# Inverse roots of the norms element by element on every partition, instead of column sums, a Newton chain on eight columns and a diagonal

## The chip, the cores and the metric

The kernel runs on one core of a Trainium2 chip. The metric is the device time of one execution in microseconds; the median of three runs of the kernel before is 2151.62 us (2151.5 to 2153.11). TensorE (PE) multiplies matrices and writes its results to PSUM banks of 128 partitions by 512 float32; PEld is its weight load, which overlaps the matmuls. VectorE (DVE) and ScalarE (ACT) read those banks and do everything element by element. GpSimd (POOL) makes a few masks at the start. SyncE's queue (SP) issues nearly all transfers, some come from ACT's queue. Each engine runs its own instructions in order and waits on semaphores for the others. Products are made in float32r with operands split into a high and a low part (three matmuls for one product); a few matmuls are float32, which the trace records as two passes.

## The reference

One decoder layer on x of 2048 rows by 1024 columns, then a final norm. Every norm has the form of `rmsnorm`:

```
def rmsnorm(x, w, eps=EPS):
    inv = lax.rsqrt(jnp.mean(x * x, axis=-1, keepdims=True) + eps)
    return x * inv * w

u    = rmsnorm(x, norm_mix_w);  proj = u @ w_in          # hq, hf, hi, hg, attention q k v
mix  = [hgrn2 heads (4), sliding-window attention heads (8)]
h    = x + mix @ w_out
v    = rmsnorm(h, norm_ffn_w)
h    = h + (silu(conv(v @ w_gate)) * (v @ w_up)) @ w_down
out  = rmsnorm(h, final_norm_w)
```

The number `inv` belongs to a row of x (a token). The kernel holds x transposed, features on partitions and tokens on the free axis, so a norm needs a sum over partitions, and its result is wanted in two forms: spread over all partitions along the token axis (`invb`, to multiply a transposed product), and as a column with tokens on partitions (`rs`, to scale the product v, which comes out with tokens on partitions).

## The kernel before, in words

The 2048 tokens are done in two halves of 1024. Each half goes through: the products k and v of attention (`kv`, two `unit`s of 48 matmuls), an interleaved stretch of HGRN2 heads and attention heads (`hgrn`, `attend`, `project_v`, in the order of the list `ORDER`), the output projection (`out_proj`, tiles `pop`), the gated MLP (`gate_up`, pairs of units by a Strassen-Winograd scheme in `pair_unit`, tiles X, Y, Z), and the down projection (`down`, tiles `pdx`, `pdy`), at whose end the next half's x is loaded (`load`) and its `kv` units begin. Around all of it a planner with a cost model of each instruction sorts the program into one order per engine; code that is written in one place can stand elsewhere in the order, and `tc.issue_after` pins some of it.

`Stats` holds the norms. Its accumulator `acc` (tiles `invb` or `sums`, 128 partitions by 1024 or 512 tokens) takes the squares of the features: ACT squares, DVE adds (line 251). Then, in before:

- `inverse` (from line 262): for each block of 128 tokens a float32 matmul with the accumulator's block as weights and one column of ones as the moving side gives 128 sums in one column of a bank `pst` (line 271); `rsqrt` (lines 169 to 181) makes the inverse root of those 8 (or 4) columns by a bit trick and three Newton steps, 11 small DVE instructions; line 279 multiplies the identity matrix by the columns, which puts 128x128 diagonals into the accumulator.
- `spread` (line 289): a float32 matmul of a matrix of ones with those diagonals puts each inverse root on all partitions (bank `pinv`), and ACT copies it to SBUF (line 292).

This happens nine times for whole, half or quarter accumulators: x of the first half (in `head`), h of each half (in `gate_up`, at products S4 and A22 of the first pair), the final norm of the first half's two column halves (`o2` while the down projection's last product P4 runs, `o` in the next half's `kv` units), x of the second half (`xs`, in the same units), and the second half's final norm at the very end (`o2`, `o`, `o`). ACT's functions live in tables, and a change to another table is an instruction of its own (`ACT_TABLE_LOAD`); Identity, Copy and Square run under any.

PSUM is handed out from three groups: `mm` (4 banks), `hg` (2) and `at` (2). Line 196 makes the low part `wlo` of a weight tile, which the third of each three matmuls of a `unit` needs. Line 1201 scales the finished output tiles h before line 1202 writes them out. Line 716 scales the product v by `rs`.

Of the kernel before, what the change touches and what calls it, by code (L numbers as in the profile page):

```python
# [8 lines left out]
F32 = mybir.dt.float32  # L9
# [31 lines left out]
UT = 7  # L41
# [12 lines left out]
def hymba_layer(ctx: ExitStack, tc: tile.TileContext, a: dict, out: bass.AP):  # L54
# [18 lines left out]
    def ps(kind, name):  # L73
        return spaces[kind].tile([P, 512], F32, tag=kind, name=name)
# [160 lines left out]
    class Stats:  # L235
# [26 lines left out]
        def inverse(self, keep, last=None):  # L262
# [12 lines left out]
            if last is not None:  # L275
# [4 lines left out]
                                    ident.unsqueeze(1).to_broadcast([P, nt, P]),  # L280
                                    rs.unsqueeze(2).to_broadcast([P, nt, P]), op=ALU.mult)

        def spread(self, bank=None):

            n = self.acc.shape[-1]
            w = min(n, 512)
            for b in range(n // w):
                pb = ps(aux[b % 2 if bank is None else bank], "pinv")[:, 0:w]
                marks["pinv"] = nc.tensor.matmul(pb, ones, self.acc[:, b * w:(b + 1) * w], start=True, stop=True)
                if bank is not None:  # L290
                    return pb
                nc.scalar.copy(self.acc[:, b * w:(b + 1) * w], pb)
# [25 lines left out]
    def head(X):  # L318


        st = Stats(inv_tile())
        raw = [raw4(None) for _ in range(3)]
        W = [tuple(wp.tile([P, D], F32R, tag=t, name=f"w{t}", bufs=2) for t in ("hi", "lo")) for _ in range(2)]
        xt = [slot("x") for _ in range(KT)]
        k0, k1, k2 = slice(0, P), slice(P, 4 * P), slice(4 * P, D)
        v0, v1 = slice(0, 2 * P), slice(2 * P, D)
        nc.sync.dma_start(raw[0][:, k0], a["w_att"][ATT_J][:, k0])
        for c in (k1, k2):
            fetched = nc.scalar.dma_start(raw[0][:, c], a["w_att"][ATT_J][:, c])
        with tc.issue_after(fetched.ins):  # L330
            nc.scalar.activation(warm, ones[:, 0:1], AF.Sigmoid)
        for kt in range(KT):
            for c in [h for _, h in halves()] if kt == 0 else [slice(0, HALF)]:
                nc.sync.dma_start(xt[kt][:, c], a["xT"][kt, :, c])
            if kt == 1:
                nc.sync.dma_start(raw[1], a["w_att"][ATT_J + 1])
        nc.sync.dma_start(raw[2], a["w_f"][0])
        o = [[ps("mm", f"kv{b}") for b in range(NB)] for _ in range(2)]
        on_act, on_pe = [], []

        def turn(f, *args):

            with tc.issue_after(on_act[-1].ins) if on_act else ExitStack():
                on_act.append(f(*args))

        def tile_of_x(kt):
            X.append(new_x())
            for c in [h for _, h in halves()] if kt == 0 else [slice(0, HALF)]:
                turn(split_w, xt[kt][:, c], nmw[:, kt:kt + 1], [t[:, c] for t in X[kt]])

        def split_w(src, w, dst):
            h, l = dst
            r = nc.scalar.activation(h, src, AF.Identity, scale=w)
            nc.vector.scalar_tensor_tensor(l, src, w, h.bitcast(F32), op0=ALU.mult, op1=ALU.subtract)
            return r

        def step(u, kt):

            hi, lo = [t[:, kt * P:(kt + 1) * P] for t in W[u]]
            xh, xl = X[kt]  # L360
            with tc.issue_after(on_pe[-1].ins) if on_pe else ExitStack():
                for w, x, f, l in ((hi, xh, kt == 0, False), (hi, xl, False, False), (lo, xh, False, kt == KT - 1)):
                    for b, bs in halves():
                        r = nc.tensor.matmul(o[u][b], w, x[:, bs], start=f, stop=l)
                on_pe.append(r)

        turn(cut, *W[0], raw[0], k0)
        tile_of_x(0)
        step(0, 0)
        turn(cut, *W[0], raw[0], k1)  # L370
        tile_of_x(1)
        step(0, 1)
        turn(cut, *W[0], raw[0], k2)
        turn(cut, *W[1], raw[1], v0)
        for kt in range(2):
            step(1, kt)
        for kt in range(2, KT):
            tile_of_x(kt)
            if kt == 2:
                turn(cut, *W[1], raw[1], v1)  # L380
            else:
                turn(st.square, xt[kt - 3])
            for u in range(2):
                step(u, kt)
        F = tuple(hp.tile([P, D], F32R, tag="m", name=f"w{t}", bufs=KT) for t in ("hi", "lo"))
        turn(cut, *F, raw[2], slice(0, D))
        for kt in range(KT - 3, KT):
            turn(st.square, xt[kt])
        summed = st.last
        with tc.issue_after(on_act[-1].ins), tc.issue_after(summed.ins):  # L390
            constants()
        with tc.issue_after(on_pe[-1].ins):
            st.inverse("x")
        with tc.issue_after(marks["pst"].ins):
            f0 = unit(F, X, "f", kind="aux", then={4: st.spread}, behind={4: "pinv"})
        return o, st.acc, st.rs, f0, summed

    def first_unit(X, i, then={}, kind="mm"):
        return unit(a["w_att"][ATT_J + i], X, "kv", kind=kind, then=then)
# [544 lines left out]
    def gate_up(hf, ops, hs, nxt, last, p):  # L944

        acts = {op: [dp.tile([P, n, 512], F32, name=f"act{hf}{op}{i}") for i, n in enumerate(PIECES)] for op in OPS}
        lo, hi = slice(0, 512), slice(512, HALF)
        invb = hs.acc
        srcs = [w[2 * pr:2 * pr + 2] for pr in range(FT // 2) for w in (a["w_gate"], a["w_up"])]
        for pr in range(FT // 2):  # L950
            f0 = 2 * pr
# [14 lines left out]
            def flush():  # L966
                while later:
                    later.pop(0)()

            later = []  # L970
            then = {"S4": lambda: hs.inverse("h"), "A22": lambda: (hs.spread(), flush())} if pr == 0 else {}
            if pr == 0:
                def behind_first(copied):
                    nonlocal nxt
# [50 lines left out]
    def down(hf, kept, acts, p):  # L1025
# [4 lines left out]
        lo, hi = slice(0, 512), slice(512, HALF)  # L1030
        final = hf + 1 == NH
        NP = len(PIECES)
        todo = [(name, w, t, j) for name, w, t in PRODUCTS for j in range(NP)]
        S = {}

# [79 lines left out]
        for k, (name, _, _, j) in enumerate(todo):  # L1115
            if k + 2 < len(todo):
                ready[k + 2] = prep_piece(k + 2)
            if j == 0:
                if name == "P1":
                    bx = o = [ps("mm", "pdx") for _ in range(4)]  # L1120
                elif name in ("P5", "P2"):
                    by = o = [ps(aux[d % 2], "pdy") for d in range(4)]
                else:
                    o = by if name == "P3" else bx
                if name == "P3":
                    acc = inv_tile() if final else wp.tile([P, HALF], F32, tag="raw", name="sums", bufs=RAW)
                    s1, s2 = [Stats(acc[:, bs], lambda: p.tile([P, 512], F32, tag="ut", name="fsq", bufs=UT))
                              for bs in (lo, hi)]
                if name == "P2" and not final:
                    stage = iter(("xh2", "xl2") * (KT // 2))  # L1130
                    loading = load(hf + 1, X, lambda: p.tile([P, HALF], F32, tag=next(stage), name="x", bufs=6))
            if not final and k >= end - 3:
                xs = next(loading, xs)
            if final and k == end:
                break
            if k == end + 1:
                s2.inverse("o2")
            elif k == end + 3:
                s2.spread()
                finish(hf, hh, s2, hi, [nc.sync])  # L1140
            for d in range(4):
                product(k, o[d], d)
            if j + 1 < NP:
                continue
            for d in range(4):
                h1, h2 = hh[d], hh[d + 4]
                if name in ("P1", "P2"):
                    add(h1[:, lo], o[d])
                elif name in ("P6", "P3"):
                    add(h1[:, hi], o[d])  # L1150
# [12 lines left out]
        if final:  # L1163
# [26 lines left out]
            steps[1][0].inverse("o", last)  # L1190
            finish(hf, hh, steps[1][0], steps[1][1], [nc.scalar, nc.sync], steps[1][0].spread(1))
            return None
        kv = [first_unit(X, 0, {3: lambda: s1.inverse("o"), 7: lambda: xs.inverse("x")}, "aux")]
        kv.append(first_unit(X, 1, {2: lambda: (s1.spread(), finish(hf, hh, s1, lo, [nc.sync])), 4: xs.spread}))
        f0 = unit(a["w_f"][0], X, "f")
        return X, kv, xs.acc, xs.rs, f0

# [103 lines left out]
```

## Time and profile before

| | |
|---|---|
| median of 3 runs | 2151.62 us (2151.5 to 2153.11) |
| the profiled execution's own time | 2152.56 us |
| its span (first to last instruction) | 2150.8 us |
| PE busy | 2136.1 us, 99% of the span |
| DVE busy | 1662.3 us, 77% |
| ACT busy | 1091.3 us, 51% |
| granted TensorE clock, mean | 0.999 |
| DMA, mean busy share of 16 engines | 34.5% on SP's queue, 0.8% on ACT's |

In rows of a timeline the columns are the start in us, the length in us (of all instructions merged into the row), engine, line, operation, output<-inputs, the shape of the array, of the moving side and type, and how many were merged; in brackets stands the idle time of the engine before it and what ended it. Matmuls overlap: a row's length is longer than the distance to the next row's start, and it is the distance that counts. The rows that carry the argument stand in the prediction.

### The profile page before, as it was taken

The numbers are of one execution on the slowest core, as the hardware profiler recorded it, in microseconds if no ns is written. First come the engines' busy times: TensorE is split into PE (matmuls) and PEld (weight loads), VectorE is DVE, ScalarE is ACT, GpSimd is POOL, SyncE is SP. The second block draws the span as 40 slices with busy tenths as digits, with TensorE's granted clock in tenths as the row PEclk, the third lists the DMA queues.
The fourth block names the chain that finished last, engine by engine and source line by source line (L and its number), as shares of the span: only waits on it lengthen the run. The fifth ranks groups of instructions, "written<-read, shape, count | busy, mean of one in ns | idle before, by whom it ended". The sixth has DMA issues, their size and how long they took to land.

```text
span 2150.8 us, 28224 instructions
## 1 busy us (share of the span) xinstructions
PE 2136.1 (99%) x10752; PEld 1786.6 (83%) x10752; DVE 1662.3 (77%) x2450; ACT 1091.3 (51%) x1858; POOL 6.0 (0%) x28
## 2 busy tenths in 40 slices
PE   9999999999999999999999999999999999999998
PEld 7888888888888888888888888888888888888888
DVE  6557888798887878785864688878978788887766
ACT  6456566564444445335734576646544444443353
POOL 1000000000000000000000000000000000000000
PEclk9999999999999999999999999999999999999999
DMA  4111112513232235964631111215223323269643
GB/s 158 49 40 40 42 37 69 164 48 132 86 126 93 97 114 171 380 222 157 214 129 41 46 42 40 64 38 174 84 93 101 110 91 122 92 205 398 224 137 133
DMA packets 94383, 258.04 MB, mean 120 GB/s; under 512 B 11416, under 2 KB 17576, under 8 KB 94248
## 3 DMA queue, kind: packets, MB, share of 16 engines
q1 hardware_dynamic: 88992, 251.30, 34.5%
q10 hardware_dynamic: 5256, 4.94, 0.8%
q8 instruction: 84, 1.38, 0.3%
q14 instruction: 51, 0.42, 0.1%
HBM read 195.10 MB, written 57.15 MB: 117 GB/s over the span
## 4 chain that ended last, share of the span: by engine, by line
PE 79%; ACT 2%; DVE 2%; issue 1%; DMA 0%; ACTq 0%; DVEq 0%
PE X L896 7%; PE X L898 7%; PE X L897 7%; PE pop L217 6%; PE pdx L1109 4%; PE pdx L1107 4%; PE Y L898 4%; PE Y L897 4%; PE Y L896 4%; PE pdx L1108 4%; PE pdy L1109 3%; PE pdy L1108 3%; PE pdy L1107 3%; PE f L217 2%; PE hq L217 2%; PE q L217 2%
## 5 line engine op out<-in xcount | busy, mean ns | idle before, releaser
L721 ACT CAST whi<-raw 128x1024 fp32r<-128x1024 f32 x88 | 92.6, 1053 | 110.3 <-PE X L897 67.6
L897 PE MATMUL X<-T,whi 128*128 128x512 f32 x352 | 137.0, 389 | 0.0
L896 PE MATMUL X<-T,whi 128*128 128x512 f32 x352 | 137.0, 389 | 0.0
L898 PE MATMUL X<-T,wlo 128*128 128x512 f32 x352 | 136.9, 389 | 0.0
L991 DVE SCALAR_TENSOR_TENSOR y<-ga,cw,y 128x1024 f32<-128x1024 f32 x88 | 112.3, 1277 | 26.0 <-ACT y L989 25.9
L903 ACT COPY u<-X 128x512 f32<-128x512 f32 x88 | 51.4, 584 | 133.0 <-PE X L898 132.6
L722 DVE TENSOR_TENSOR wlo<-raw,whi 128x1024 fp32r<-128x1024 f32 x88 | 107.0, 1215 | 0.0
L195 ACT CAST whi<-raw 128x1024 fp32r<-128x1024 f32 x57 | 59.7, 1051 | 87.1 <-PE hq L217 37.1
L196 DVE TENSOR_TENSOR wlo<-raw,whi 128x1024 fp32r<-128x1024 f32 x57 | 69.4, 1217 | 43.3 <-ACT whi L195 42.8
L722 DVE TENSOR_TENSOR xld<-raw,xhd 128x1024 fp32r<-128x1024 f32 x72 | 80.5, 1129 | 19.8 <-ACT xhd L721 19.4
L721 ACT CAST xhd<-raw 128x1024 fp32r<-128x1024 f32 x72 | 69.6, 977 | 43.5 <-DMA raw<-act0T 13.9
L217 PE MATMUL pop<-XL,whi 128*128 128x512 f32 x256 | 88.6, 392 | 0.0
L217 PE MATMUL pop<-XH,wlo 128*128 128x512 f32 x256 | 87.7, 391 | 0.0
L217 PE MATMUL pop<-XH,whi 128*128 128x512 f32 x256 | 86.4, 393 | 0.0
L897 PEld LDWEIGHTS X<-T,whi 128*128 128x128 f32 x352 | 66.1, 188 | 13.7
L898 PEld LDWEIGHTS X<-T,wlo 128*128 128x128 f32 x352 | 66.1, 188 | 13.7
L896 PEld LDWEIGHTS X<-T,whi 128*128 128x128 f32 x352 | 66.0, 188 | 13.7
L1107 PE MATMUL pdx<-xhd,hid 128*128 128x512 f32 x192 | 74.5, 392 | 1.6 <-ACT hid L721 1.0
L619 DVE TENSOR_TENSOR QK<-QK,f 128x1024 f32<-128x1024 f32 x56 | 68.5, 1224 | 8.1 <-ACT G L605 7.7
L1108 PE MATMUL pdx<-xld,hid 128*128 128x512 f32 x192 | 74.7, 389 | 0.0
L1109 PE MATMUL pdx<-xhd,lod 128*128 128x512 f32 x192 | 73.8, 389 | 0.0
L896 PE MATMUL X<-T,Sh 128*128 128x512 f32 x176 | 68.7, 391 | 1.5 <-ACT s L903 1.5
(385 smaller groups left out, 6413.1 us busy)
## 6 DMA issues: line engine op xcount, KB each, us to landing
wr<-in_w_down SPq DMA_DIRECT2D x90, 512.0 KB, 5.4
raw<-in_w_gate SPq DMA_DIRECT2D x44, 512.0 KB, 3.7
raw<-in_w_up SPq DMA_DIRECT2D x44, 512.0 KB, 3.6
raw<-act0T SPq DMA_DIRECT2D x20, 512.0 KB, 8.2
raw<-act1T SPq DMA_DIRECT2D x20, 512.0 KB, 8.3
act0B<-y SPq DMA_DIRECT2D x33, 256.0 KB, 3.2
act1B<-y SPq DMA_DIRECT2D x33, 256.0 KB, 2.3
raw<-in_w_out SPq DMA_DIRECT2D x16, 512.0 KB, 5.1
```

Of the source, the lines that this page charges most:

```text
L196: nc.vector.tensor_tensor(lo, raw, hi.bitcast(F32), op=ALU.subtract)
L217: marks["unit"] = nc.tensor.matmul(o[b], w, x[:, bs], start=f, stop=l)
L619: done = nc.vector.tensor_tensor(own, own, Fv.rearrange("p b w -> p w b").unsqueeze(3).to_broadcast([P, 2, nb, m]), op=ALU.mult)
L721: return (nc.scalar.copy(h, src), (eng or nc.vector).tensor_tensor(l, src, h.bitcast(F32), op=ALU.subtract))
L722: (eng or nc.vector).tensor_tensor(l, src, h.bitcast(F32), op=ALU.subtract))
L896: nc.tensor.matmul(o, wh[:, ws], xh, start=i == 0 and not more, stop=False, skip_group_check=more)
L897: nc.tensor.matmul(o, wh[:, ws], xl, start=False, stop=False, skip_group_check=more)
L898: r = nc.tensor.matmul(o, wl[:, ws], xh, start=False, stop=i == 3, skip_group_check=more)
L991: nc.vector.scalar_tensor_tensor(y, g[:, w:w + HALF], C.cw[:, ft, w:w + 1], y, op0=ALU.mult, op1=ALU.add)
L1107: nc.tensor.matmul(o, wh[:, i, c], ah[:, i, cols], start=f, stop=False, skip_group_check=more)
L1108: nc.tensor.matmul(o, wh[:, i, c], al[:, i, cols], start=False, stop=False, skip_group_check=more)
L1109: nc.tensor.matmul(o, wl[:, i, c], ah[:, i, cols], start=False, stop=l, skip_group_check=more)
```

## The change

Two new functions of `Stats`. `everywhere` replaces `inverse` and `spread` in six of the nine places (x, h of both halves, and `o2`, `o` and `xs` between the halves; the last three at the program's end stay as they were). For each block of 512 tokens: one float32 matmul of ones with the accumulator itself gives the sums on all partitions (bank `psum`), ACT reads the bank and makes the inverse root of every element by a table function (`Abs_reciprocal_sqrt`), DVE reads the bank for the scaled sum, ACT squares the root, and two DVE instructions do one Newton step and leave the result in the accumulator. The planner makes DVE's read of the bank (line 300) wait for ACT's (line 299). `column` makes the column form `rs` for v: it writes partition 0 of the result to DRAM (4 KB) and reads it back with tokens on partitions, 128 partitions by 8 numbers of 4 bytes each. Line numbers in after are 22 to 30 higher from there on.

```diff
+        def column(self):
+            n = self.acc.shape[-1]
+            rs = self.rs = sp.tile([P, n // P], F32, tag="rs", name="rs")
+            row = dp.tile([1, n], F32, name="row")
+            nc.sync.dma_start(row, self.acc[0:1])
+            nc.sync.dma_start(rs, row.rearrange("o (c t) -> (o t) c", t=P))
+
+        def everywhere(self, part, kinds):
+            n = self.acc.shape[-1]
+            for b in range(n // 512):
+                a = self.acc[:, b * 512:(b + 1) * 512]
+                s = ps(kinds[b % 2], "psum")
+                marks["psum"] = nc.tensor.matmul(s, ones, a, start=True, stop=True)
+                y, t = part("y"), part("t")
+                nc.scalar.activation(y, s, AF.Abs_reciprocal_sqrt, scale=1.0 / D, bias=eps)
+                nc.vector.tensor_scalar(a, s, -0.5 / D, -0.5 * EPS, op0=ALU.mult, op1=ALU.add)
+                nc.scalar.activation(t, y, AF.Square)
+                nc.vector.tensor_tensor(t, t, a, op=ALU.mult)
+                nc.vector.scalar_tensor_tensor(a, t, 1.5, y, op0=ALU.add, op1=ALU.mult)
...
         with tc.issue_after(on_pe[-1].ins):
-            st.inverse("x")
-        with tc.issue_after(marks["pst"].ins):
-            f0 = unit(F, X, "f", kind="aux", then={4: st.spread}, behind={4: "pinv"})
+            st.everywhere(lambda name: slot(name)[:, 0:512], aux)
+            st.column()
+        with tc.issue_after(marks["psum"].ins):
+            f0 = unit(F, X, "f", kind="aux")
...
-            then = {"S4": lambda: hs.inverse("h"), "A22": lambda: (hs.spread(), flush())} if pr == 0 else {}
+            then = {"S4": lambda: hs.everywhere(ring, ("mm", "mm")), "A22": flush} if pr == 0 else {}
...
             if k == end + 1:
-                s2.inverse("o2")
+                s2.everywhere(ring, aux)
             elif k == end + 3:
-                s2.spread()
                 finish(hf, hh, s2, hi, [nc.sync])
...
-        kv = [first_unit(X, 0, {3: lambda: s1.inverse("o"), 7: lambda: xs.inverse("x")}, "aux")]
-        kv.append(first_unit(X, 1, {2: lambda: (s1.spread(), finish(hf, hh, s1, lo, [nc.sync])), 4: xs.spread}))
+        kv = [first_unit(X, 0, {3: lambda: s1.everywhere(ring, aux), 7: lambda: (xs.everywhere(ring, aux), xs.column())}, "aux")]
+        kv.append(first_unit(X, 1, {2: lambda: (finish(hf, hh, s1, lo, [nc.sync]))}))
```

Counted over the program, PE loses 40 of its 50 `pst` matmuls on columns of ones and turns 10 `pinv` matmuls into 10 `psum` matmuls of the same shape; ACT loses 10 copies of 128x512 and gains 10 inverse roots, 10 squares and 5 table loads (38 instead of 33); DVE loses 66 small instructions and the diagonals (line 279, four of 128x1024 and two of 128x512) and gains 30 of 128x512; SP gains 4 transfers.

The order moves in three places that the prediction speaks of. First PE in the head, behind the last `kv` matmul (tile `f` is the first HGRN2 unit); before:

```order
L364 MATMUL kv_144<-XH,wlo 128x512
L364 MATMUL kv_145<-XH,wlo 128x512
L271 MATMUL pst<-ones,invb 128x1 x8
L217 MATMUL f_385<-XH,whi 128x512
L217 MATMUL f_386<-XH,whi 128x512
```

and now:

```order
L386 MATMUL kv_144<-XH,wlo 128x512
L386 MATMUL kv_145<-XH,wlo 128x512
L297 MATMUL psum<-invb,ones 128x512 x2
L217 MATMUL f_383<-XH,whi 128x512
L217 MATMUL f_384<-XH,whi 128x512
```

The two sums over all partitions stand where the eight columns stood, and the two `pinv` matmuls that stood after 24 of the 48 `f` matmuls are gone. ACT at the same place (`lbe` is a small softmax for the forget gates, `kT` and `vT` get their bias after DVE has scaled them); before:

```order
L195 CAST whi<-raw 128x1024 x2
L156 ACT_TABLE_LOAD
L156 ACTIVATE lbe<-lbe 128x8
L292 COPY invb<-pinv 128x512 x2
L419 ACTIVATE kT<-kT,battn 128x512
L419 ACTIVATE vT<-vT,battn 128x512
```

and now:

```order
L195 CAST whi<-raw 128x1024 x2
L299 ACT_TABLE_LOAD
L299 ACTIVATE y<-psum,warm 128x512
L156 ACT_TABLE_LOAD
L156 ACTIVATE lbe<-lbe 128x8
L301 ACTIVATE t<-y 128x512
L299 ACT_TABLE_LOAD
L299 ACTIVATE y<-psum,warm 128x512
L301 ACTIVATE t<-y 128x512
L442 ACTIVATE kT<-kT,battn 128x512
L442 ACTIVATE vT<-vT,battn 128x512
```

The exponential for `lbe` stands between the two roots, so there are three table loads where there was one. Then DVE shortly before the second half's `kv` units (`gad` is the last weight piece of the down projection, `h ... sums` the scaling of finished output, `XL` a low part of x, `wlo` the low part of the first `kv` unit's weights); before:

```order
L722 TENSOR_TENSOR gad<-wr,gad 128x512
L232 SCALAR_TENSOR_TENSOR XL<-x,nmw,XH 128x1024
L179 TENSOR_TENSOR t<-y 128x4
L251 TENSOR_TENSOR invb<-invb,x 128x1024
L180 TENSOR_TENSOR t<-t,ms 128x4
L196 TENSOR_TENSOR wlo<-raw,whi 128x1024
```

and now:

```order
L745 TENSOR_TENSOR gad<-wr,gad 128x512
L1230 TENSOR_TENSOR h_7160<-h_7160,sums 128x512
L1230 TENSOR_TENSOR h_7162<-h_7162,sums 128x512
L1230 TENSOR_TENSOR h_7164<-h_7164,sums 128x512
L1230 TENSOR_TENSOR h_7166<-h_7166,sums 128x512
L1230 TENSOR_TENSOR h_7168<-h_7168,sums 128x512
L1230 TENSOR_TENSOR h_7170<-h_7170,sums 128x512
L1230 TENSOR_TENSOR h_7172<-h_7172,sums 128x512
L1230 TENSOR_TENSOR h_7174<-h_7174,sums 128x512
L232 SCALAR_TENSOR_TENSOR XL<-x,nmw,XH 128x1024
L251 TENSOR_TENSOR invb<-invb,x 128x1024
L196 TENSOR_TENSOR wlo<-raw,whi 128x1024
```

The eight scalings of `o2`, which followed the `kv` unit's start before, now stand ahead of that unit's `wlo`. On SP the two transfers of `column` stand behind the third of four loads of `w_v` in the head and behind the second in the second half; and the eight output writes of `o2` now stand ahead of the second half's loads of `w_f` and `w_q`. In the MLP and the down projection's beginning the planner sorts many rows anew (which of two ready products PE takes first), with the same instructions.

More of the change, by code (lines that the diff above doesn't have):

```diff
@@ L948, in gate_up, with ring @@
         invb = hs.acc
+        def ring(name):
+            return p.tile([P, 512], F32, tag="ut", name=name, bufs=UT)
         srcs = [w[2 * pr:2 * pr + 2] for pr in range(FT // 2) for w in (a["w_gate"], a["w_up"])]
@@ L1032, in down, with ring @@
         NP = len(PIECES)
+        def ring(name):
+            return p.tile([P, 512], F32, tag="ut", name=name, bufs=UT)
         todo = [(name, w, t, j) for name, w, t in PRODUCTS for j in range(NP)]
```

## The prediction

> **What bounds the kernel now.** First the page, then the busy times by stretch, then the rows around each norm. Page, parts 1 and 2:
>
> ```profile
> span 2150.8 us, 28224 instructions
> PE 2136.1 (99%) x10752; PEld 1786.6 (83%) x10752; DVE 1662.3 (77%) x2450; ACT 1091.3 (51%) x1858; POOL 6.0 (0%) x28
> PEclk9999999999999999999999999999999999999999
> ```
>
> PE works 2136.1 of 2150.8 us at an unthrottled clock. Only time on PE counts: what an edit takes out of PE's order is gained, what makes PE wait is lost. Busy times by stretch (its length, then each engine's time and instructions) for the first MLP and the `kv` units between the halves:
>
> ```profile
> 445.00:860.00 415.00, 414.27 (x1832) 342.27 (x1831) 347.93 (x451) 186.96 (x269) 0.00 (x0) 1.00 0.34 110
> 1070.00:1100.00 30.00, 30.00 (x140) 24.20 (x139) 22.86 (x55) 8.50 (x12) 0.00 (x0) 1.00 0.40 141
> ```
>
> PE idles 0.73 of 415 us in the MLP and none of 30 where the next half begins. The sums by columns therefore lie on the path, with nothing that hides them. The head's PE rows, none with an idle time in brackets:
>
> ```profile
> 30.91 1.84 PE L271 MATMUL pst<-ones,invb 128*128 128x1 f32 x16
> 32.61 0.72 PE L217 MATMUL f<-XH,whi 128*128 128x512 f32 x2
> 33.17 0.63 PE L217 MATMUL f<-XL,whi 128*128 128x512 f32 x2
> 33.64 0.62 PE L217 MATMUL f<-XH,wlo 128*128 128x512 f32 x2
> 34.09 0.62 PE L217 MATMUL f<-XH,whi 128*128 128x512 f32 x2
> ...
> 38.20 1.88 PE L289 MATMUL pinv<-invb,ones 128*128 128x512 f32 x4
> 39.51 1.03 PE L217 MATMUL f<-XH,whi 128*128 128x512 f32 x2
> 40.38 0.62 PE L217 MATMUL f<-XL,whi 128*128 128x512 f32 x2
> ```
>
> Two `f` matmuls take 0.455 (33.64 to 34.09), one 0.227. From 30.91 to 33.17 lie eight `pst` matmuls (16 records) and two `f`: the eight cost 2.26 - 0.455 = **1.80**. From 38.20 to 40.38 two `pinv` and two `f`: 2.18 - 0.455 = 1.73 for a pair. Half an accumulator, at the second half's start:
>
> ```profile
> 1077.03 1.02 PE L289 MATMUL pinv<-sums,ones 128*128 128x512 f32 x2
> 1077.48 0.79 PE L217 MATMUL kv<-XH,whi 128*128 128x512 f32 x1
> 1078.11 0.40 PE L217 MATMUL kv<-XL,whi 128*128 128x512 f32 x1
> ...
> 1082.88 0.95 PE L271 MATMUL pst<-ones,sums 128*128 128x1 f32 x8
> 1083.69 0.49 PE L217 MATMUL kv<-XL,whi 128*128 128x512 f32 x1
> 1084.02 0.40 PE L217 MATMUL kv<-XH,wlo 128*128 128x512 f32 x1
> ```
>
> Four `pst` cost 1.14 - 0.23 = **0.91**, a single `pinv` 1.08 - 0.23 = 0.85.
>
> **The change, part by part.** *PE.* Removed are 40 `pst` matmuls: eight each for x, h, h and xs, four each for `o2` and `o`: 4 x 1.80 + 2 x 0.91 = **9.0 us**, at places without a PE wait. The ten `psum` have the shape of the ten `pinv` and the same grouping (pairs for x and h, singles for `o2`, `o`, xs): 0.
>
> *The MLP's wait.* PE stands still once per half in the first MLP pair:
>
> ```profile
> 459.55 0.39 PE L898 MATMUL X<-B,wlo 128*128 128x512 f32 x1
> 460.67 0.50 PE L896 MATMUL X<-T,Sh 128*128 128x512 f32 x1 [0.73 <-ACT s L903]
> PE X L896 <- ACT s L903: 1.5, 2, 0.7
> ```
>
> The product S2T2 goes on in bank X, which ACT must copy first, and nothing stands between. In the new order ten Z and two Y matmuls stand there, 12 x 0.227 = 2.7 us, more than the copy needs: **-1.5** in all. Bounds: 0 if another wait takes its place, -1.5.
>
> *Head, ACT and DVE.* The roots are made later than PE's `f` begins, so the question is whether `vT` and the `kv` banks are ready when `f` ends.
>
> ```profile
> 30.65 1.05 ACT L195 CAST whi<-raw 128x1024 fp32r<-128x1024 f32 x1 [0.30 <-PE kv L364]
> 31.72 1.28 ACT L156 ACT_TABLE_LOAD   x1
> 33.01 0.21 ACT L156 ACTIVATE lbe<-lbe 128x8 f32<-128x8 f32 x1
> 39.25 0.58 ACT L292 COPY invb<-pinv 128x512 f32<-128x512 f32 x1 [6.03 <-PE pinv L289]
> 41.23 0.71 ACT L419 ACTIVATE vT<-vT,battn 128x512 f32<-128x512 f32 x1
> 39.87 0.69 DVE L418 TENSOR_TENSOR kT<-kv,invb 128x512 f32<-128x512 f32 x1 [3.02 <-ACT invb L292]
> ```
>
> ACT read a `pinv` bank 1.05 after its matmul began (39.25 - 38.20), so the first `psum` is there at 31.96. A pass of 512 columns costs ACT 0.58 to 0.71; the new root has no row, I take 0.65 and 0.6 for the square. Then: load to 33.24, root 33.9, load 35.2, `lbe` 35.4, square 36.0, load 37.3, root 37.95, square 38.55. DVE, at 0.65 an instruction, waits for ACT at each step and reaches the first `kT` at 40.1, beside 39.87 before; the first `vT` has its bias at 42.1. PE, with the pair done at 30.91 + 1.73, ends `f` at 32.64 + 48 x 0.227 = 43.5 and takes `vT` then: 1.4 us to spare, so **0**. If the root costs twice the row, the slack is still not used up.
>
> *h.* Per half ACT works 1.28 + 2 x 1.25 - 2 x 0.58 = 2.6 us more, DVE makes six passes of 512 in place of eleven small instructions and the diagonal. The same stretch shows what hides it:
>
> ```profile
> 454.59 0.59 ACT L903 COPY u<-X 128x512 f32<-128x512 f32 x1 [4.99 <-PE X L898]
> 465.22 2.50 DVE L962 TENSOR_TENSOR ga<-ga,invb 128x512 f32<-128x512 f32 x4 [2.75 <-ACT invb L292]
> ```
>
> ACT had 4.99 us idle there and DVE stood 2.75 us waiting for the spread root, which now comes without a second trip over PE: **0**. Line 300, which waits for ACT's load and root, holds up on DVE the low parts of the last T4 operand and of the next unit's weights; in the new order both are due some 5 us later on PE. Were the cover gone, the `Sl` of the second unit would be late next, whose turn on PE I put 2.8 us after it is ready.
>
> *Between the halves.* Here the cover is thin. DVE scales `o2`'s eight output tiles ahead of the weights of the first `kv` unit:
>
> ```profile
> 1059.13 2.19 ACT L231 ACTIVATE XH<-x,nmw 128x1024 fp32r<-128x1024 f32 x2 [3.26 <-DMA x<-in_xT]
> 1062.79 0.68 DVE L722 TENSOR_TENSOR gad<-wr,gad 128x512 fp32r<-128x512 f32 x1
> 1066.65 1.23 DVE L196 TENSOR_TENSOR wlo<-raw,whi 128x1024 fp32r<-128x1024 f32 x1 [0.26 <-ACT whi L195]
> 1071.36 0.39 PE L217 MATMUL kv<-XH,whi 128*128 128x512 f32 x1
> 1078.70 4.90 DVE L1201 TENSOR_TENSOR h<-h,sums 128x512 f32<-128x512 f32 x8 [0.76 <-ACT sums L292]
> ```
>
> The table load and root put ACT's casts 1.9 us back; its 3.26 us of waiting for x swallow that, and I put `gad`'s end at 64.3 (63.5 before). Then 4.9 for `h` and three passes of 128x1024 (`XL`, `invb`, `wlo`) at 1.2, as long as the `wlo` row: `wlo` is ready at 1072.8. PE starts `kv` at 1071.3 and needs it at the fifth matmul, 1072.2. A wait of about **+0.5**; bounds 0 (casts not pushed back) and 2 (the whole push of 1.9 arrives). Behind it the chain is shorter than before: two trips over PE are one, so `kv`'s banks come free before `hq` asks for them, and `w_f` and `w_q` wait about 2 us behind eight writes but are cast 12 us later: 0.
>
> *Column form.* SP stands still until the root is made, writes, waits for the landing, and reads; behind it wait the loads of the last `w_v` pieces and of `w_g`. In the head that is from about 42 to 46, in the second half from about 1101.
>
> ```profile
> L716 ACT ACTIVATE v<-pvv,y x16: 677/687/702, 80.7 to 1183.5; 128x512 f32<-128x512 f32 x16
> 26.36 34.27 SPq L187 DMA_DIRECT2D raw<-in_w_v  x4
> 1145.48 0.69 ACT L716 ACTIVATE v<-pvv,y 128x512 f32<-128x512 f32 x1 [0.43 <-PE pvv L715]
> q10 hardware_dynamic: 5256, 4.94, 0.8%
> odd<-moved ACTq DMA_DIRECT2D x8, 112.0 KB, 2.3
> ```
>
> First use is at 80.7 and 1145.5; the fourth `w_v` load goes out only at 60.6 anyway. ACT's queue moved 5256 packets in 0.8% of 16 x 2150.8 us, 52 ns each; 1024 pieces of 4 bytes at that price take 3.3 us over 16 engines: **0**.
>
> *Sum.* -9.0 - 1.5 + 0.5, and +0.6 for a wait like the MLP's that the new order may bring elsewhere (estimate: one of 0.73): **-9.4**. The profiled execution took 2152.56, so 2143.2; it stood 0.94 above the median, so **2142.2** against 2151.62. With its bounds: -11 (MLP's wait gone, no new one) to -7 (2 at `kv`, 2 elsewhere): 2140.6 to 2144.6.
>
> **Rivals.** *Late chains* (ACT and DVE late at the head and at `kv`): the covers are 1.4 us in the head and none at `kv`. If the root takes ACT as long as a load (1.28) and each hand-over costs 0.3, two roots and six hand-overs make 1.3 + 1.8 = 3.1 late, 1.7 waited in the head, and 2 more at `kv`: 2142.2 + 3.7 = **2146**. For it: strict order on DVE, where line 300 waits for ACT. Against: the copy that ends at 39.83 releases `kT` at 39.87, a hand-over of 0.04.
>
> [...]
>
> *The planner's new order eats the gain.* It was sorted for other durations; in the first MLP PE idles 0.73 us of 415, so the old order left nothing. If the reordered third of each MLP (four pairs and the change to the down projection) brought a 0.73 wait in six places per half, 8.8 us go: **2151**. Against: the order before, by the same planner, had one.
>
> *Slower: the 4-byte read stands in a line.* If its 1024 pieces run on one engine instead of 16, 52 ns x 1024 = 53 us, the column lands at about 98 and 1156 instead of before 80.7 and 1145.5; ACT, in order, stands still at line 716 some 17 and 15 us, PE soon after behind full banks. At 15 each: 2142.2 + 30 = **2172**. It decides from some 35 us of landing on. Against: 112 rows of 1 KB landed in 2.3 us, so a transfer with partitions outermost does spread. [...]
>
> **How the numbers follow.** Forecast 0.72, late chains 0.13, drain 0.03, eaten gain 0.07, slow read 0.05. 0.2% (4.3 us, about what this measurement tells from no change) is passed below 2147.3. Faster: 0.70 of the forecast, 0.11 of the late chains, 0.03 of the drain, 0.84; same: 0.02, 0.02 and 0.06 of the eaten gain, 0.10; slower: its last 0.01 and the slow read's 0.05. The range, 2139.5 to 2147.5, takes in the forecast's bounds and the late chains.
>
> **What would show it.** Right: PE busy about 2127, no `pst` before the tail, 38 table loads, the wait on `s` gone in the first pair of both MLPs, a short PE wait for `wlo` at `kv`. Wrong: PE waits in the head for `vT` or a `kv` bank (late chains; ACT gaps after the loads: the drain), waits scattered over the MLP, or ACT idle before the scaling of v for want of `rs` (slow read).

## The result: 0.24% slower, with the time lost in the pace of matmuls that the change does not touch

The changed kernel takes 2157.57 us in the median of 11 runs (2156.53 to 2158.7); the kernel before, run beside it, 2152.59 us (11 runs, 2151.5 to 2153.73). The ratio is 1.0024, 95% interval 1.0015 to 1.0033. Forecast were 2142.2 us, a gain of 9.4; the range ended at 2147.5. It came out 5 us slower instead, some 15 us beside the forecast.

The page of the changed kernel, parts 1 and 2, and the first stretch that the prediction showed of before (length, then busy time and instructions of PE, PEld, DVE, ACT, POOL, granted clock, DMA share, GB/s):

```profile
span 2156.6 us, 28063 instructions
PE 2143.6 (99%) x10672; PEld 1778.8 (82%) x10672; DVE 1666.3 (77%) x2408; ACT 1104.2 (51%) x1873; POOL 6.4 (0%) x28
PEclk9999999999999999999999999999999999999999
...
445.00:860.00 415.00, 414.24 (x1799) 337.25 (x1798) 346.68 (x442) 188.25 (x270) 0.00 (x0) 1.00 0.33 110
```

PE has 80 records fewer (40 float32 matmuls of two passes each), as the change says, and yet 7.5 us more busy time. In the MLP it is as busy as before, 414.24 of 415 us at clock 1.00, and gets through 1799 matmuls where it got through 1832. (Eight of the 33 fewer come with the change of instructions and of their places in the order: the same instructions at the old addresses, below, have 1824. The other 25 are lost pace.) So no wait took the gain; the matmuls themselves follow each other more slowly. PE's waits of the changed kernel (line waited for: us in total, times, longest) agree:

```profile
PE pdx L1137 <- ACT xhd L744: 1.3, 2, 0.8
...
PE kv L217 <- DVE wlo L196: 0.3, 1, 0.3
```

The two waits of 0.73 for `s` are gone, the short one for `wlo` has come (0.3 where 0.5 was forecast), and nothing on the list is near 15 us.

Where the pace is lost shows when groups of one operation are laid side by side (busy us, mean ns of one). First before, then the changed kernel:

```profile
L896 PE MATMUL X<-B,whi 128*128 128x512 f32 x176 | 68.5, 389 | 0.0
L896 PE MATMUL Y<-T,Sh 128*128 128x512 f32 x176 | 68.5, 389 | 0.0
L897 PE MATMUL X<-T,Sh 128*128 128x512 f32 x176 | 68.5, 389 | 0.0
```

```profile
L919 PE MATMUL X<-B,whi 128*128 128x512 f32 x176 | 69.3, 394 | 0.0
L919 PE MATMUL Y<-T,Sh 128*128 128x512 f32 x176 | 69.3, 394 | 0.0
L920 PE MATMUL X<-T,Sh 128*128 128x512 f32 x176 | 68.7, 391 | 0.0
```

The same three products, the same shape and count: two take 394 ns instead of 389, the third 391. A matmul has two operands, its weights and its moving operand; here the moving operand is a block of the MLP's input (B) or a sum of blocks (T), of which the rows give the letter alone. The slow ones are those whose moving operand (B11, T1, B21) lies in the pool that is opened for the MLP, its "second homes"; the operands T2, T3, T4 and B22 lie in the first homes, the pool of x. The sum needs the distance between starts rather than the length. A stretch of product Y (start us, length us) in the changed kernel:

```profile
599.66 0.39 PE L919 MATMUL Y<-T,Sh 128*128 128x512 f32 x1
599.89 0.40 PE L920 MATMUL Y<-T,Sh 128*128 128x512 f32 x1
600.13 0.39 PE L921 MATMUL Y<-T,Sl 128*128 128x512 f32 x1
600.36 0.40 PE L919 MATMUL Y<-T,Sh 128*128 128x512 f32 x1
600.60 0.39 PE L920 MATMUL Y<-T,Sh 128*128 128x512 f32 x1
600.83 0.40 PE L921 MATMUL Y<-T,Sl 128*128 128x512 f32 x1
601.06 0.39 PE L919 MATMUL Y<-T,Sh 128*128 128x512 f32 x1
601.29 0.40 PE L920 MATMUL Y<-T,Sh 128*128 128x512 f32 x1
```

Seven distances make 1.63 us, 233 ns each, where the prediction reckoned with 227.

What differs is an address, that is, the byte at which a tile starts in each partition of SBUF, the memory in which the kernel's tiles lie. The new code needs fewer small tiles (the column roots of x, h and the final norm go, the column form `rs` comes), so the pool `small` shrinks from 768 to 640 bytes a partition, and each pool opened after it starts 128 bytes earlier. In the built programs the second homes start at byte 141120 before (64 modulo 256) and at 140992 in the changed kernel (192 modulo 256); first homes and weights stay at 64 modulo 256 in both (weights that lie in a second home move with it). Of the 8340 float32r matmuls of 512 columns, 48 have a moving operand and weights that are not a multiple of 256 bytes apart before the change, and 2172 after it.

### The profile page after: what moved, and what is told of

It reads as the page before. It is cut to its first block, busy times and chain, and to the rows that moved or that the text cites. A ratio compares the mean times of both kernels' runs of the same rounds, so it can differ in the third digit from the quotient of the medians.

```text
span 2156.6 us, 28063 instructions
## 1 busy us (share of the span) xinstructions
PE 2143.6 (99%) x10672; PEld 1778.8 (82%) x10672; DVE 1666.3 (77%) x2408; ACT 1104.2 (51%) x1873; POOL 6.4 (0%) x28
## 2 busy tenths in 40 slices
DMA packets 96466, 258.04 MB, mean 120 GB/s; under 512 B 13498, under 2 KB 19658, under 8 KB 96332
## 4 chain that ended last, share of the span: by engine, by line
PE 80%; ACT 1%; DVE 1%; DMA 1%; issue 0%; ACTq 0%; DVEq 0%
PE X L920 7%; PE X L919 7%; PE X L921 7%; PE pop L217 6%; PE Y L920 4%; PE Y L919 4%; PE Y L921 4%; PE pdx L1137 3%; PE pdx L1139 3%; PE pdx L1138 3%; PE pdy L1137 3%; PE pdy L1138 3%; PE pdy L1139 3%; PE q L217 2%; PE f L217 2%; PE g L217 2%
## 5 line engine op out<-in xcount | busy, mean ns | idle before, releaser
L920 PE MATMUL Z<-B,whi 128*128 128x512 f32 x176 | 69.5, 395 | 0.0
```

The source lines that it names most:

```text
L920: nc.tensor.matmul(o, wh[:, ws], xl, start=False, stop=False, skip_group_check=more)
```

## The experiments

Three theories were open. **Placement:** a 512-column matmul is slower when its moving operand and its weights are not a multiple of 256 bytes apart. **Order:** the planner's new order of the matmuls costs PE its pace. **Contention:** the added ACT work and table loads do. In each kernel with a widened tile every engine's instructions stand in the same order as in the kernel that it was made from, and nothing is computed differently.

### The changed kernel, put back on its old addresses

```diff
-        ms = sp.tile([P, n], F32, tag=f"ms{n}", name="ms")
+        ms = sp.tile([P, n + 16 * (n == 8)], F32, tag=f"ms{n}", name="ms")[:, 0:n]
```

> The changed kernel with one tile of the small pool widened by 64 bytes a buffer (two buffers), so that the pools opened after it, the second-home operands of the MLP among them, start 128 bytes later: at the address that they had before the change. Every engine's instructions stand in the same order as in the changed kernel. Placement theory (a 512-column matmul is slower when its moving operand and its weights stand 128 bytes apart modulo 256; 2172 such matmuls in the changed kernel, 48 before): each goes back from about 233 to 226.7 ns from start to start, 2172 x 6.5 ns = 14.1 us less, 2157.6 - 14.1 = 2143.5 us, which is also the forecast of the prediction (2142.2) within 1.5 us; the MLP products of the page fall from 390 to 389 ns a matmul. Rival, order theory (the planner's new order of the matmuls is what costs PE its pace): the order is the same, so the time stays 2157.6 us. Rival, contention theory (the added ACT work and table loads take the pace from PE): 2157.6 us too.

Measured: 2142.01 us (5 runs, 2141.48 to 2142.64) beside 2152.05 of before (20 runs); ratio 0.9953, interval 0.9939 to 0.9966. Its page, its MLP stretch, the groups of above, and the same stretch of product Y:

```profile
span 2140.1 us, 28063 instructions
PE 2127.5 (99%) x10672; PEld 1778.2 (83%) x10672; DVE 1666.2 (78%) x2408; ACT 1105.6 (52%) x1873; POOL 6.0 (0%) x28
...
445.00:860.00 415.00, 414.27 (x1824) 342.02 (x1823) 352.46 (x449) 191.66 (x274) 0.00 (x0) 1.00 0.35 114
...
L919 PE MATMUL X<-B,whi 128*128 128x512 f32 x176 | 68.5, 389 | 0.0
L919 PE MATMUL Y<-T,Sh 128*128 128x512 f32 x176 | 68.5, 389 | 0.0
...
597.72 0.39 PE L920 MATMUL Y<-T,Sh 128*128 128x512 f32 x1
597.95 0.39 PE L921 MATMUL Y<-T,Sl 128*128 128x512 f32 x1
598.17 0.39 PE L919 MATMUL Y<-T,Sh 128*128 128x512 f32 x1
598.40 0.39 PE L920 MATMUL Y<-T,Sh 128*128 128x512 f32 x1
598.63 0.39 PE L921 MATMUL Y<-T,Sl 128*128 128x512 f32 x1
598.85 0.39 PE L919 MATMUL Y<-T,Sh 128*128 128x512 f32 x1
599.08 0.39 PE L920 MATMUL Y<-T,Sh 128*128 128x512 f32 x1
599.31 0.39 PE L921 MATMUL Y<-T,Sl 128*128 128x512 f32 x1
```

Seven distances now make 1.59 us, 227 ns each. 128 unused bytes give 15.6 us (2157.57 - 2142.01), with the same instructions in the same order: the order and contention theories fall. This is also the version that beats both kernels.

### The kernel before, moved off its addresses

The same edit on the kernel before.

> The kernel before with the same widening and nothing else: its operands move 128 bytes later, to where 2172 of the 512-column matmuls have moving operand and weights 128 bytes apart modulo 256. Placement theory: 2124 more such matmuls x 6.5 ns = 13.8 us more, 2152.6 + 13.8 = 2166.4 us, with the MLP's windows losing the pace that they lose in the changed kernel. Order theory and contention theory: no instruction is added or moved, so 2152.6 us.

Measured: 2168.05 us (4 runs, 2167.5 to 2169.21), ratio 1.0074, interval 1.006 to 1.0088: 16.0 us slower, the other two theories' 2152.6 excluded. Its page and its MLP stretch:

```profile
span 2166.5 us, 28224 instructions
PE 2152.1 (99%) x10752; PEld 1787.2 (82%) x10752; DVE 1663.9 (77%) x2450; ACT 1091.1 (50%) x1858; POOL 6.4 (0%) x28
...
445.00:860.00 415.00, 414.27 (x1808) 337.60 (x1807) 342.39 (x445) 183.82 (x266) 0.00 (x0) 1.00 0.32 106
```

1808 matmuls against 1832, at the same busy time. 16.0 us over 2124 matmuls more are 7.5 ns each, over the 6.5 expected; where the rest lies comes below.

### Absolute or relative: the constants moved

```diff
-        C.omlb = cp.tile([P, HG], F32, name="omlb")
+        C.omlb = cp.tile([P, HG + 32], F32, name="omlb")[:, 0:HG]
```

This edit alone on the changed kernel moves everything behind the constants by 128 bytes:

> The changed kernel with the last tile of the constants widened by 128 bytes: every pool behind the constants starts 128 bytes later. The second-home operands are then at the very address that they had before the change, but the weights and the first-home operands have moved by the same 128 bytes, so that 2220 matmuls still have moving operand and weights 128 bytes apart modulo 256. Theory of the relative place (weights against moving operand): no gain, 2157.6 us (2172 to 2220 such matmuls, +0.3 us). Theory of the absolute place (a start at 192 modulo 256 is slow for a moving operand, a start at 64 is quick, whatever the weights): the 1896 matmuls on second-home operands become quick, but the 6444 on first-home operands and on weights used as moving operand become slow, 2157.6 + (6444 - 1896) x 6.5 ns = 2187 us. Theory that only the second homes' own place matters: back to 2143.5 us.

Measured: 2156.91 us (10 runs, 2156.41 to 2159.88), ratio 1.0024, interval 1.0015 to 1.0033. The second homes are at the very address of before, and nothing is gained. Then both edits together:

> The changed kernel with both widenings: the last constant by 128 bytes and the small pool by 128 bytes. First homes, weights and second homes all start at 192 modulo 256; all 8340 matmuls of 512 columns have moving operand and weights a multiple of 256 bytes apart, and not one stands at the place modulo 256 that it had before the change. Theory of the relative place: 2157.6 - 2172 x 6.5 ns = 2143.5 us, as the kernel with the old addresses (2142.0). Theory of the absolute place (192 modulo 256 is slow for a moving operand): all 8340 are slow, 2142.0 + 8340 x 6.5 ns = 2196 us; a theory by which only the second homes' own place or the weights' own place matters gives 2157 us.

Measured: 2142.53 us (5 runs, 2141.96 to 2143.97) beside 2152.6 of before, ratio 0.9954, interval 0.9941 to 0.9968. Everything stands at 192 modulo 256, and the kernel is as fast as with everything at 64. The page's first lines of the two, constants alone and then both:

```profile
span 2155.6 us, 28063 instructions
PE 2142.9 (99%) x10672; PEld 1777.8 (82%) x10672; DVE 1666.3 (77%) x2408; ACT 1104.3 (51%) x1873; POOL 6.0 (0%) x28
```

```profile
span 2140.6 us, 28063 instructions
445.00:860.00 415.00, 414.08 (x1823) 341.82 (x1823) 352.71 (x449) 191.62 (x274) 0.00 (x0) 1.00 0.34 114
```

With that the four corners are measured, and of these theories only that of the relative place fits all four:

| changed kernel | second homes at 64 modulo 256 | second homes at 192 |
|---|---|---|
| weights and first homes at 64 | 2142.01 | 2157.57 |
| weights and first homes at 192 | 2156.91 | 2142.53 |

### Half the distance

The first edit with 8 in place of 16: 64 bytes in all, second homes at 0 modulo 256.

> The changed kernel with the small pool widened by 64 bytes in all: the second-home operands start at 0 modulo 256 and the weights at 64, 64 bytes apart. This is for the size of the step. If any distance other than a multiple of 256 costs the same: 2157.6 us. If the distance counts in steps of 64 bytes and half the distance costs half: about 2150.5 us. If 64 bytes apart is as good as none: 2143.5 us.

Measured: 2156.77 us (9 runs, 2155.85 to 2158.64), ratio 1.002, interval 1.0011 to 1.003. By the total any distance costs the same. But seen as moving operand minus weights, 1752 of the 2220 displaced matmuls stand at 192 here and only 468 at 64, so the total says little about 64. The starts in the traces, each matmul of the MLP and the down projection matched to the addresses of its operands, tell it finer (mean distance to the next start, distances under 300 ns):

| moving operand minus weights, modulo 256 | MLP | down projection | from |
|---|---|---|---|
| 0, all operands so placed | 226.7 ns | 226.7 to 226.9 ns | before, and both placed kernels |
| 128, moving operand in a second home | 232.6 ns (x1560) | 232.4 ns (x190) | changed kernel |
| 128, weights in a second home | 232.7 ns (x24) | 232.9 ns (x396) | changed kernel |
| 192, moving operand in a second home | 233.3 ns (x1560) | 233.3 ns (x190) | 64 bytes |
| 64, weights in a second home | 230.8 ns (x24) | 228.9 ns (x396) | 64 bytes |
| 0, among such matmuls | 227.9 ns (x2082) | 227.3 ns (x1050) | changed kernel |

So it is not the same for all: a distance of 64 costs 2 to 4 ns, 128 and 192 some 6. At 128 it makes no difference which of the two has moved; at 64 and 192 that was not separated, since in these two stretches 64 is always a matter of moved weights and 192 of a moved operand. The step is 256 bytes and not 512: in the kernel before, the second homes stand an odd multiple of 256 from their weights (141120 - 91200 = 195 x 256) and the first homes an even one, and both go at 226.4 to 227.0 ns. The last row is the rest that the 6.5 ns left out: well-placed matmuls behind displaced ones lose a little too. In the MLP it is the first five behind one, 231.3, 233.0, 230.3, 228.0 and 227.4 ns in their order; from the sixth on they take 226.6 to 226.9, and so does one in front of a displaced one (226.9). For the changed kernel the table gives 1584 x 6.0 + 586 x 6.1 + 2082 x 1.2 + 1050 x 0.6 = 16.2 us, measured 15.6.

### The parts of the change, each put back on a placed kernel

To see whether the sum's own terms were right, one part at a time goes back to the old way, with the pool widened so that the placement is that of before. For h:

```diff
-            then = {"S4": lambda: hs.everywhere(ring, ("mm", "mm")), "A22": flush} if pr == 0 else {}
+            then = {"S4": lambda: hs.inverse("h"), "A22": lambda: (hs.spread(), flush())} if pr == 0 else {}
```

> The changed kernel with the norm in front of the MLP (h) made in the old way again, x and the final norm in the new way, and the small pool widened by 64 bytes so that all 8292 matmuls of 512 columns have moving operand and weights a multiple of 256 bytes apart, as before the change. By the terms of the prediction: two groups of eight column matmuls come back, 2 x 1.80 = 3.6 us, and the two waits of PE for the first S operand, 1.5 us: 2142.0 + 5.1 = 2147.1 us. Rival (the terms of the sum are right in total by accident, and the gain of the placed kernel comes from the planner's order): the part of h need not be half of the 10; anything between 2142 and 2152 us, and the waits for s do not come back with it.

Measured: 2147.51 us (11 runs), ratio 0.9979 (0.997 to 0.9987). For x, in the head and between the halves:

```diff
-            st.everywhere(lambda name: slot(name)[:, 0:512], aux)
-            st.column()
+            st.inverse("x")
...
-        with tc.issue_after(marks["psum"].ins):
-            f0 = unit(F, X, "f", kind="aux")
+        with tc.issue_after(marks["pst"].ins):
+            f0 = unit(F, X, "f", kind="aux", then={4: st.spread}, behind={4: "pinv"})
...
-        kv = [first_unit(X, 0, {3: lambda: s1.everywhere(ring, aux), 7: lambda: (xs.everywhere(ring, aux), xs.column())}, "aux")]
-        kv.append(first_unit(X, 1, {2: lambda: (finish(hf, hh, s1, lo, [nc.sync]))}))
+        kv = [first_unit(X, 0, {3: lambda: s1.everywhere(ring, aux), 7: lambda: xs.inverse("x")}, "aux")]
+        kv.append(first_unit(X, 1, {2: lambda: (finish(hf, hh, s1, lo, [nc.sync])), 4: xs.spread}))
```

> The changed kernel with the norm of x made in the old way again in both halves (column matmuls, vector root, diagonal, spread by ones; no column form by DRAM), h and the final norm in the new way, and the small pool widened by 128 bytes for the same placement as before the change. By the terms of the prediction: two groups of eight column matmuls, 3.6 us, less the waits of 0.5 us for the low weights at the second half's first unit: 2142.0 + 3.1 = 2145.1 us. Rival (the new form of x costs something near its own gain, by its table loads and its float32 rows on ACT and DVE): 2142 us or below.

Measured: 2145.8 us (6 runs), ratio 0.9971 (0.996 to 0.9982). For the first half's final norm:

```diff
-                s2.everywhere(ring, aux)
+                s2.inverse("o2")
             elif k == end + 3:
+                s2.spread()
...
-        kv = [first_unit(X, 0, {3: lambda: s1.everywhere(ring, aux), 7: lambda: (xs.everywhere(ring, aux), xs.column())}, "aux")]
-        kv.append(first_unit(X, 1, {2: lambda: (finish(hf, hh, s1, lo, [nc.sync]))}))
+        kv = [first_unit(X, 0, {3: lambda: s1.inverse("o"), 7: lambda: (xs.everywhere(ring, aux), xs.column())}, "aux")]
+        kv.append(first_unit(X, 1, {2: lambda: (s1.spread(), finish(hf, hh, s1, lo, [nc.sync]))}))
```

> The changed kernel with the first half's final norm made in the old way again (two groups of four column matmuls), x and h in the new way, and the small pool widened by 64 bytes for the same placement as before the change. By the terms of the prediction: 2 x 0.91 = 1.8 us come back: 2142.0 + 1.8 = 2143.8 us. The three parts together: 5.1 + 3.1 + 1.8 = 10.0 us, what the placed kernel gained over the kernel before. Rival (the final norm's new form sits beside work that waits anyway): 2142 us.

Measured: 2143.69 us (5 runs), ratio 0.9959 (0.9947 to 0.9972). Above 2142.01 the three stand 5.5 (expected 5.1), 3.8 (3.1) and 1.7 us (1.8); together 11.0 where the placed kernel gained 10.0. The first two are clear of the spread of the runs. The third is not: its runs (2142.1 to 2144.17) overlap those of the placed kernel (2141.48 to 2142.64), so the rival of 2142 us is not excluded by the time. The wait for `s` comes back with h, here first, as expected; the row behind it is from the kernel with the old x:

```profile
PE X L919 <- ACT s L926: 1.5, 2, 0.7
```

```profile
PE kv L217 <- DVE wlo L196: 1.2, 1, 1.2
```

The second row goes against what was expected of that kernel: the wait for `wlo` does not leave with the new form of x. Its length, 1.2 here and 0.3 in the placed kernel, says little: two other kernels with the placed kernel's order of instructions have 0.4 (both widenings) and 1.0 (the next section's). It is the kernel with the old final norm whose trace has no such wait. DVE's timeline shows why, in the placed kernel and then in the one with the old final norm:

```profile
1060.04 4.89 DVE L1230 TENSOR_TENSOR h<-h,sums 128x512 f32<-128x512 f32 x8
...
1068.92 1.21 DVE L196 TENSOR_TENSOR wlo<-raw,whi 128x1024 fp32r<-128x1024 f32 x1
```

```profile
1066.21 1.22 DVE L196 TENSOR_TENSOR wlo<-raw,whi 128x1024 fp32r<-128x1024 f32 x1
...
1073.96 4.91 DVE L1231 TENSOR_TENSOR h<-h,sums 128x512 f32<-128x512 f32 x8 [1.34 <-ACT sums L314]
```

With the new form of `o2` its eight output tiles are scaled ahead of the unit's weights, as the prediction had it; with the old one the scaling stands behind them. The wait was put to the wrong part in the expectation. Without it the part of x is 3.6, against 3.8 measured, and that of the final norm 1.8 less the wait of 0.3 or more, against 1.7; these runs do not resolve a few tenths.

### A second place where operands stand apart

The attention scores' keys and queries stand 64 bytes apart modulo 256 in the placed kernel. One small tile of the mixing stretch, widened, takes that away:

```diff
-                F = p.tile([P, nb], F32, tag="F", name="F", bufs=2)
+                F = p.tile([P, nb + 24], F32, tag="F", name="F", bufs=2)[:, 0:nb]
```

> The placed kernel (the changed kernel with the pools back at their old addresses, 2142.0 us) with a small tile of the mixing stretch widened by 96 bytes a buffer, so that from there on the stretch's tiles start 192 bytes later: the query operands of the attention scores move from 64 bytes beside the keys modulo 256 to no distance. The 256 matmuls of 256 columns there have 118 ns from start to start (median) and would have 227 / 2 = 113 if their place is what slows them: 256 x 5 ns = 1.3 us less, 2140.7 us. The float32 matmuls of 128 columns that move with them stand at 112 ns with and without a distance now, so nothing is expected there. Rival (the 118 ns come from waits and from the heads' alternation, not from the place): 2142.0 us and 118 ns.

Measured: 2142.55 us (5 runs, 2141.97 to 2143.72), ratio 0.9957 (0.9943 to 0.997): no gain. Half of the score matmuls in the placed kernel, then here:

```profile
L487 PE MATMUL psc<-KS,qh 128*128 128x256 f32 (+1 forms) x128 | 33.1, 290 | 0.0
```

```profile
L487 PE MATMUL psc<-KS,qh 128*128 128x256 f32 (+1 forms) x128 | 33.3, 291 | 0.0
```

From start to start the median is 118 ns apart and 119 together. The theory was carried too far: at 256 columns the place shows no cost. The down projection's 256-column matmuls say the same at a greater distance: 119 to 120 ns at 128 in the changed kernel, 120 to 121 at 0 in the placed one. The float32 matmuls of 128 columns that moved too kept their 112 ns.

## Why the prediction was wrong, step by step

**The step that failed** is the first: "Only time on PE counts: what an edit takes out of PE's order is gained, what makes PE wait is lost." From it the sum took two kinds of terms, instructions removed and waits, and took it that a matmul which the change leaves alone keeps its 226.7 ns. 2172 of them did not (some 233 ns), and the well-placed ones close behind them lost a little: 15.6 us, without a wait and without an instruction, from 128 bytes that a pool no longer holds. No rival had a mechanism of this kind, and so the range, 2139.5 to 2147.5, left the measured 2157.57 out. The diff showed that a pool that others follow would change its size (a tile tag more and several fewer). That this sets the pace of matmuls could not be read from the groups of before, where all but 48 of the 8340 stood well.

**The terms that the sum did have** hold on the old addresses: the placed kernel takes 2142.01 us where 2142.2 were forecast, and PE is busy 2127.5 us in it, where the prediction named 2127 as a sign. That the times agree to 0.2 us is in part luck. The gain was 10.0 where 9.4 was forecast, from 2152.05 where the sum began at 2151.62; and in the profiled executions PE's busy time fell by 8.6 and its idle time by 2.1, where the terms make 9.0 and 0.4.

- 40 column matmuls, -9.0, and two waits for `s`, -1.5: the parts of x, h and the final norm cost 3.8, 5.5 and 1.7 us when put back, where these terms give 3.6, 5.1 and 1.8, the last less the next point and within the spread of its runs.
- `wlo` at the second half's first unit, +0.5: the wait is there, 0.3 in the changed kernel and 0.3 to 1.0 in the kernels placed well. It goes with the new form of `o2`, as the prediction's working had it, and not with x.
- The allowance of +0.6 for a new wait: one of that size did come, 0.7 for `xhd` at `pdx` in the placed kernel, but others there went with it. `hid` fell from 1.0 to 0.6 and `y` from 0.5 to nothing, and no wait but `wlo` was added elsewhere, so in sum nothing was to be paid.
- The bounds, -11 to -7, do not come out of the terms named with them: -9.0 and -1.5 make -10.5, and with 2 us at `kv` and 2 elsewhere -6.5. The measured loss of 5 us lies outside either way.
- Head, 0. ACT and DVE of the changed kernel:

```profile
31.89 1.28 ACT L299 ACT_TABLE_LOAD   x1 [0.31 <-PE psum L297]
33.19 0.69 ACT L299 ACTIVATE y<-psum,warm 128x512 f32<-128x512 f32 x1
33.89 1.28 ACT L156 ACT_TABLE_LOAD   x1
35.19 0.21 ACT L156 ACTIVATE lbe<-lbe 128x8 f32<-128x8 f32 x1
...
39.90 0.68 DVE L441 TENSOR_TENSOR kT<-kv,invb 128x512 f32<-128x512 f32 x1
```

  The root takes 0.69 (0.65 was taken), the first `kT` starts at 39.90 (40.1 reckoned, 39.87 before), and PE doesn't wait there. That excludes late chains in the head. No run shows the drain (ACT gaps after the loads) that has 0.03 of the chances: in these rows a load takes 1.28 us, the first starts when its bank is there and the second 0.01 after the root's end, and the next instruction starts 0.02 after either. Of the trace's 38 loads 29 are followed within 0.02 us, the other nine by an instruction that waits for DVE.
- Column form, 0. The two transfers go out at 41.81 and 43.04, and v is scaled from 78.7 on with PE as what ACT waited for; no row shows a wait for `rs`. Packets under 512 bytes rise from 11416 to 13498, by 2082, which is twice the 1024 pieces that the prediction counted and 34 more; with the old form of x they are 11416 again.

```profile
41.81 0.30 SPq L288 DMA_DIRECT2D row<-invb  x1
43.04 0.39 SPq L289 DMA_DIRECT2D rs<-row  x1
L739 ACT ACTIVATE v<-pvv,rs x16: 687/689/704, 78.7 to 1184.7; 128x512 f32<-128x512 f32 x16
  PE pvv L738: 35.8, 13
```

**The rivals.** Late chains, drain and slow read didn't occur. The eaten gain (2151, scattered waits from the planner's order) came nearest in time but for another reason: on the same order, with 128 bytes added, all of the gain is there.

## What to carry to other kernels

When a change adds or drops a tile, compare the addresses of all that lies behind it, and keep moving operand and weights of the 512-column matmuls a multiple of 256 bytes apart: here 128 unused bytes were worth 15.6 us, more than the change itself. When a kernel's waits don't explain its time, count the matmuls in a window where PE is busy throughout, and mind what else changed in the window: 1824 against 1799 in 415 us, with the same instructions, is lost pace, and then the groups' mean times say for which operands. A timed change to a tuned kernel can hold a placement of its own, so judge the change on placements that are alike (2152.05 to 2142.01 here, or 2168.05 to 2157.57, either way 10 us).

## What the hardware showed that was not expected

In these kernels the distance of moving operand and weights modulo 256 bytes sets the pace of a float32r matmul of 512 columns that has a weight load for each: 226.7 ns at 0, 229 to 231 at 64 (weights moved), 232.4 to 232.9 at 128, 233.3 at 192 (moving operand moved). At 128 it is the same whichever of the two was moved (232.4 to 232.6 with the moving operand moved, 232.7 to 232.9 with the weights), and at 256 columns no cost was seen (118 ns from start to start at 64 and 119 at 0 in the scores, 119 to 120 at 128 and 120 to 121 at 0 in the down projection). Why the distance counts is not shown: the weight loads themselves take 188 ns in both kernels, and whether it is the distance from the matmul's own weights or from the next one's that counts was not separated, since neighbours nearly always had the same place. One sign points to the next one's. The down projection has 26 well-placed matmuls right in front of one whose weights stand 128 off; they take 232.7 ns in the changed kernel and 226.0 at the same spots in the placed one, while in the MLP a well-placed one in front of a displaced moving operand loses nothing (226.9). With weights 64 off the same 26 spots show no loss (226.0), so the question stays open.
